# Token-major blocks computed in pairs of 512 columns, with the forward states scanned early, in an encoder layer of neighbourhood attention and gated linear attention

## The chip, the cores and the metric

The kernel runs on one core of a Trainium2 chip. The metric is the device time of one execution in microseconds. PE is TensorE, DVE is VectorE, ACT is ScalarE, POOL is GpSimd, SP is SyncE, whose queue issues nearly all DMAs.

## What is computed

One layer of a hybrid encoder for two sequences, a prompt P of 512 tokens and a sample S of 1024, in fp32, width 1024. The normalized input u is projected by one matrix w_in into eleven parts; the parts that matter here are

```
proj = u @ w_in + b_in
na_q, na_k, na_v (512 columns each)        # neighbourhood attention, 8 heads
gla_q, gla_k (256 each), gla_v, gla_g (512 each)   # gated linear attention, 4 heads
gate_na, gate_gla (1024 each)

# gated linear attention, forwards and (flipped) backwards, per head
state = chunk_decay * state + k_dec^T v          # one state per chunk of tokens
o     = (scores within the chunk) v + q_dec state
gla_o = rmsnorm(o) * silu(gla_g)
```

Neighbourhood attention, the two output projections, their gating, the output matrix and a squared-relu MLP follow.

## The kernel before

**Exactness.** Every matmul of a projection is done as three: each operand x is split into a rounded high part (ACT, `Ring.split` L51 or `split_act` L153) and a remainder (DVE, L52 or L154), and high x high, high x low and low x high are summed in psum.

**Two ways of projecting.** A channel-major unit (`dense_cm`, L225 to L227) holds 128 columns of weights as the stationary operand and streams 512 tokens: 24 matmuls of N = 512. A token-major unit (`dense_tm` with `tm_half`, L250 to L252) holds 128 tokens and streams a block of 256 weight columns: 24 matmuls of N = 256, for each of the 12 groups of 128 tokens (0 to 3 are P, 4 to 11 are S; 10 and 11 are done together). The token-major blocks in the stage are numbered: 4 and 5 are the two halves of gla_g, 1 the second half of gla_v, 2 and 3 the two halves of na_v.

**What follows a token-major unit**, `out_tm`: DVE adds the bias row out of psum into an sbuf tile `sv` (L316; the tag has two buffers). Block 1 is stored as it is. Blocks 2 and 3 are split into high and low (ACT L153, then DVE L154) into a tile `svr` or `svl`, one buffer each, chosen by the token group, and stored by two DMAs. Blocks 4 and 5 pass a silu on ACT (L332) and a multiplication on POOL (L334) and are stored to glag_d (L335). All of these DMAs are issued by SP.

**The weights** come through `Ring`: SP loads a [128x1024] raw tile (two buffers), ACT and DVE split it into a high and a low tile (three buffers each).

**The stage.** The list `mid` (L825 to L831) holds the units in their order: block 4, the channel-major weights k1 (the keys of the second pair of heads), blocks 1, 5, 2, 3, then the projections na (24 units) and the gates (24 units here). `run_dense` (L343 to L361) walks through it with a clock by hand: each group of three matmuls adds its cost (0.65 for N = 512, 0.325 for N = 256), and each time the clock passes 3.9 times the value that was last yielded, it lets the side generator `gla_all` issue its next piece. A finished unit's evacuation is issued a little later (`done`, `flush`).

**The side work**, `gla_all`, is the gated linear attention in two passes, one per pair of heads: segments of 512 tokens, 0P0, 0S0, 0S1, then 1P0, 1S0, 1S1. A visit to a segment (L771 to L803) is a loop over l = 0, 2, 4, 6, called a step here, each with four yields of 0.5: PE computes scores of two levels (L622; 16 matmuls a level), DVE merges them by a mask into `att` (`merge`, L660), and DVE prepares the operands Q and K of the next two levels (`ew`, L633 to L649). At the end of a segment the decayed keys are transposed (`kdt`, L694), multiplied with v into the states `st` (`upd`, L703). After the last segment of a sequence the states are chained by `scan` (L710 to L716, DVE, forward L715 and backward L716, in three thirds), and `out_mm` (L726, L727) multiplies scores and states. All of this goes into the same engines' queues in the order in which it is issued.

## Time and profile before

| | us |
|---|---|
| time, median of 3 runs (lowest to highest) | 2110.87 (2110.83 to 2110.98) |
| the profiled execution, its own time | 2112.74 |
| the profiled execution, its span | 2110.8 |
| PE busy (share of the span) | 2089.7 (99%) |
| DVE busy | 1318.2 (62%) |
| ACT busy | 974.9 (46%) |
| POOL busy | 64.5 (3%) |
| mean granted clock of PE | 0.998 |

The span is what lies between the first and the last instruction of the profile; the own time holds what lies around it too. Busy times overlap, since the engines work beside each other. The waits of an engine are told by what ended them; "L250 <- DVE sv L316" is a matmul of line 250 that waited for DVE's instruction of line 316.

### The profile page before, as it was taken

Reading aid. Unit: us, or ns where it says so; the run is one execution under the profiler, and the core shown is the slowest. Engines: PE = TensorE matmul, PEld = TensorE weight load, DVE = VectorE, ACT = ScalarE, POOL = GpSimd, SP = SyncE. Lnnn points to the kernel's source line nnn. Section 1 sums busy time; section 2 is a strip of 40 time slices with the busy share of each in tenths; the row PEclk is TensorE's granted clock in tenths of the full one; section 3 lists DMA queues with packets and bytes.
Section 4 is the critical chain, followed back from the end, with each engine's and each line's share of the span. In section 5 each row is a group of like instructions: output and inputs, shape, how many; then the busy total and the mean of one; then the engine's idle time right before and its main releaser. Section 6 shows DMA issues by size and latency. Waiting matters only on the chain.

```text
span 2110.8 us, 32043 instructions
## 1 busy us (share of the span) xinstructions
PE 2089.7 (99%) x11964; PEld 1890.3 (90%) x11964; DVE 1318.2 (62%) x2428; ACT 974.9 (46%) x1914; POOL 64.5 (3%) x92
## 2 busy tenths in 40 slices
PE   9999999999999999999999999999999999999998
PEld 8899998888888888898898999999999888888887
DVE  7465875767346666465576777997887444443544
ACT  6532232333345555452353666676666333333442
POOL 1020100000000000000000000000000000000000
PEclk9999999999999999999999999999999999999999
DMA  6342334564386776466666566766876755454643
GB/s 212 116 147 86 97 112 140 126 170 91 111 246 202 217 217 198 149 212 226 245 215 250 174 165 173 228 202 197 267 234 176 264 200 186 157 170 162 220 170 110
DMA packets 256426, 381.86 MB, mean 181 GB/s; under 512 B 35856, under 2 KB 163856, under 8 KB 256272
## 3 DMA queue, kind: packets, MB, share of 16 engines
q1 hardware_dynamic: 256128, 379.56, 57.5%
q8 instruction: 94, 1.54, 0.3%
q14 instruction: 60, 0.49, 0.1%
q10 hardware_dynamic: 144, 0.26, 0.0%
HBM read 256.02 MB, written 123.73 MB: 180 GB/s over the span
## 4 chain that ended last, share of the span: by engine, by line
PE 80%; DVE 2%; ACT 1%; DMA 1%; issue 1%; SPq 0%; POOLq 0%; DVEq 0%; ACTq 0%
PE psd L225 6%; PE psd L227 6%; PE psd L226 6%; PE psa L1426 4%; PE psa L1428 4%; PE psa L1427 4%; PE psa L1581 2%; PE psa L1580 2%; PE psa L1582 2%; PE psb L1580 2%; PE psb L1581 2%; PE psb L1582 2%; PE psc L1581 2%; PE psc L1580 2%; PE psc L1582 2%; PE psb L1428 2%
## 5 line engine op out<-in xcount | busy, mean ns | idle before, releaser
L154 DVE TENSOR_TENSOR al<-al,ah 128x1024 fp32r<-128x1024 f32 x82 | 100.2, 1223 | 145.7 <-ACT ah L153 135.2
L153 ACT ACTIVATE ah<-al 128x1024 fp32r<-128x1024 f32 x82 | 86.6, 1057 | 225.2 <-DMA al<-ads 134.3
L225 PE MATMUL psd<-uhiS,wh 128*128 128x512 f32 x448 | 179.6, 401 | 0.8 <-ACT st L287 0.8
L227 PE MATMUL psd<-uhiS,wl 128*128 128x512 f32 x448 | 175.3, 391 | 0.0
L226 PE MATMUL psd<-uloS,wh 128*128 128x512 f32 x448 | 174.8, 390 | 0.0
L1426 PE MATMUL psa<-c,uwh 128*128 128x384 f32 x512 | 171.7, 335 | 0.8 <-DVE xb L1366 0.7
L1428 PE MATMUL psa<-c,uwl 128*128 128x384 f32 x512 | 171.0, 334 | 0.0
L1427 PE MATMUL psa<-c,uwh 128*128 128x384 f32 x512 | 171.0, 334 | 0.0
L1331 DVE TENSOR_TENSOR uwl<-ux,uwh 128x512 fp32r<-128x512 f32 x192 | 131.0, 687 | 58.7 <-ACT uwh L1347 57.6
L1347 ACT ACTIVATE uwh<-ux 128x512 fp32r<-128x512 f32 x192 | 120.0, 626 | 79.6 <-DVE ux L1341 66.3
L52 DVE TENSOR_TENSOR wl<-wr,wh 128x1024 fp32r<-128x1024 f32 x70 | 85.5, 1223 | 105.2 <-ACT wh L51 94.1
L51 ACT ACTIVATE wh<-wr 128x1024 fp32r<-128x1024 f32 x70 | 73.8, 1056 | 143.9 <-PE psc L1231 66.0
L225 PEld LDWEIGHTS psd<-uhiS,wh 128*128 128x128 f32 x448 | 84.2, 188 | 18.3 <-ACT st L287 1.2
L227 PEld LDWEIGHTS psd<-uhiS,wl 128*128 128x128 f32 x448 | 84.1, 188 | 18.2
L226 PEld LDWEIGHTS psd<-uloS,wh 128*128 128x128 f32 x448 | 84.3, 188 | 16.1
L1426 PEld LDWEIGHTS psa<-c,uwh 128*128 128x128 f32 x512 | 96.1, 188 | 1.5 <-DVE xb L1366 1.0
L1427 PEld LDWEIGHTS psa<-c,uwh 128*128 128x128 f32 x512 | 96.1, 188 | 0.0
L1428 PEld LDWEIGHTS psa<-c,uwl 128*128 128x128 f32 x512 | 96.1, 188 | 0.0
L250 PE MATMUL psd<-wh,uhiS 128*128 128x256 f32 x320 | 92.7, 290 | 0.8 <-DVE sv L316 0.8
L251 PE MATMUL psd<-wl,uhiS 128*128 128x256 f32 x320 | 90.9, 284 | 0.0
L252 PE MATMUL psd<-wh,uloS 128*128 128x256 f32 x320 | 90.8, 284 | 0.0
L225 PE MATMUL psd<-uhiP,wh 128*128 128x512 f32 x224 | 90.3, 403 | 0.0
(557 smaller groups left out, 5889.4 us busy)
## 6 DMA issues: line engine op xcount, KB each, us to landing
ux<-in_wup_dram SPq DMA_DIRECT2D x64, 512.0 KB
al<-ads SPq DMA_DIRECT2D x48, 512.0 KB
al<-ad SPq DMA_DIRECT2D x34, 512.0 KB
bq<-t_d SPq DMA_DIRECT2D x64, 256.0 KB
wr<-in_wst_dram SPq DMA_DIRECT2D x28, 512.0 KB
gate_d<-st SPq DMA_DIRECT2D x48, 256.0 KB
sg<-gate_d SPq DMA_DIRECT2D x32, 384.0 KB
ad<-xa SPq DMA_DIRECT2D x64, 192.0 KB
```

What stands on the lines that cost most here:

```text
L154: V.tensor_tensor(lo, src, hi.bitcast(F32), op=ALU.subtract)
L225: T.matmul(p, wh, xh[:, k, sl], start=(k == 0), stop=False)
L226: T.matmul(p, wh, xl[:, k, sl], start=False, stop=False)
L227: T.matmul(p, wl, xh[:, k, sl], start=False, stop=(k == 7))
L1331: V.tensor_tensor(lo, usrc.pop(m - 1), hi.bitcast(F32), op=ALU.subtract)
L1347: A.activation(uhl[m][0], usrc[m], AF.Copy)
L1426: T.matmul(u[b], wh[:, es], c[:, 0, k], start=(new and k == 0), stop=False, skip_group_check=True)
L1427: T.matmul(u[b], wh[:, es], c[:, 1, k], start=False, stop=False, skip_group_check=True)
L1428: T.matmul(u[b], wl[:, es], c[:, 0, k], start=False, stop=(k == 3), skip_group_check=True)
L1580: T.matmul(p, ah[:, jj], bh[:, cs], start=((new or last) and jj == 0), stop=False, skip_group_check=True)
L1581: T.matmul(p, ah[:, jj], bl[:, cs], start=False, stop=False, skip_group_check=True)
L1582: T.matmul(p, al[:, jj], bh[:, cs], start=False, stop=(kh == 1 and jj == 7), skip_group_check=True)
```

## The change

The blocks (4, 5) and (2, 3) become two pairs (`dense_pair`): a unit holds 128 tokens and streams 512 weight columns, 24 matmuls of N = 512 (cost 0.68 per three), and when it ends, both blocks' evacuations are issued one after the other. Token groups 0 and 1 are done together, and 10 and 11. The order is k1 first, then pair (4, 5), pair (2, 3), then block 1, which stays as it was, and then the rest. The pairs' weights are loaded in sixteen pieces of [128x512] by ACT's queue, each split by `split_act` into one shared buffer: those of the first pair during k1 and in the first token groups, those of the second during the last two of the first pair (`next_pair`); in the last two of the second pair the ring is started again (`next_ring`). Ring is rebuilt on eight shared [128x1024] buffers, which the stages behind use too. The forward chain of states over the first four chunks (`scan_f`, three operations for each of two heads) is issued in the steps l = 4 and l = 6 of the second segment of S, and the scan leaves it out; its three yields go from 1.1, 0.9, 0.9 to 0.8, 0.8, 0.9. The four yields of a step go from 0.5 each to 0.46, 0.46, 0.46, 0.65. A few tiles find other places (the tile of zeros, the gate weights, the bias rows, now in three buffers).

```diff
-    def __init__(self, nc, raw, rawtag, nraw, pool, tag, nslots, items):
-        self.nc, self.raw, self.pool, self.items = nc, raw, pool, items
-        self.rawtag, self.tag, self.nraw, self.nslots = rawtag, tag, nraw, nslots
+    def __init__(self, nc, pool, nbuf, items):
+        self.nc, self.pool, self.items = nc, pool, items
+        self.free, self.limit, self.done = list(range(nbuf)), len(items), 0
         self.loaded, self.parts = [], []
+
+    def alloc(self, dt, name):
+        s = self.free.pop(0)
+        return s, self.pool.tile([128, 1024], dt, tag=f"w{s}", name=name)
 
     def load(self):
         i = len(self.loaded)
-        t = self.raw.tile([128, 1024], F32, tag=self.rawtag, bufs=self.nraw, name=f"{self.tag}r{i}")
-        self.nc.sync.dma_start(t, self.items[i])
-        self.loaded.append(t)
+        self.loaded.append(self.alloc(F32, f"wr{i}"))
+        self.nc.sync.dma_start(self.loaded[i][1], self.items[i])
 
     def split(self):
         i = len(self.parts)
-        t = self.loaded[i]
-        hi = self.pool.tile([128, 1024], F32R, tag=self.tag + "h", bufs=self.nslots, name=f"{self.tag}h{i}")
-        lo = self.pool.tile([128, 1024], F32R, tag=self.tag + "l", bufs=self.nslots, name=f"{self.tag}l{i}")
+        s, t = self.loaded[i]
+        (hs, hi), (ls, lo) = [self.alloc(F32R, f"w{c}{i}") for c in "hl"]
         self.nc.scalar.activation(hi, t, AF.Copy)
         self.nc.vector.tensor_tensor(lo, t, hi.bitcast(F32), op=ALU.subtract)
-        self.parts.append((hi, lo))
+        self.free.append(s)
+        self.parts.append((hs, ls, hi, lo))
+
+    def release(self, live):
+
+        while self.done < min(live, len(self.parts)):
+            self.free += self.parts[self.done][:2]
+            self.done += 1
 
     def fill(self, live):
 
-        n = len(self.items)
+        self.release(live)
         while True:
-            if len(self.loaded) < n and len(self.loaded) - len(self.parts) < self.nraw:
+            if len(self.loaded) < self.limit and len(self.loaded) - len(self.parts) < 2 and self.free:
                 self.load()
-            elif len(self.parts) < len(self.loaded) and len(self.parts) - live < self.nslots:
+            elif len(self.parts) < len(self.loaded) and len(self.parts) - self.done < 3 and len(self.free) > 1:
                 self.split()
             else:
                 return
 
-    def step(self, live):
-
-        if len(self.parts) < min(len(self.items), live + self.nslots):
-            if len(self.loaded) == len(self.parts):
-                self.load()
-            self.split()
-            if len(self.loaded) < len(self.items):
-                self.load()
-
     def get(self, i):
-        return self.parts[i]
+        return self.parts[i][2:]
...
-    def add_mv(b):
-        add(f"mv{b}", d["wmv"][2 * b], d["wmv"][2 * b + 1])
-
-    for n in ("q0", "k0", "q1"):
+    for n in ("q0", "k0", "q1", "k1"):
         add(n, d["wst"][ST[n]])
-    add_mv(4)
-    add("k1", d["wst"][3])
-    add_mv(1)
-    add_mv(5)
-    add_mv(2)
-    add_mv(3)
+    add("mv1", d["wmv"][0], d["wmv"][1])
     for i in range(8):
...
-    ring = Ring(nc, raw, "wraw", 2, rngp, "w", 3, items)
+    ring = Ring(nc, raw, 8, items)
+    ring.limit = where["mv1"]
...
-    zero = cst.tile([128, 128], F32, name="zero")
-    V.memset(zero, 0.0)
...
-        brow[b] = stg2.tile([128, 256], F32, tag="brow", name=f"brow{b}")
+        brow[b] = stg2.tile([128, 256], F32, tag="brow", bufs=3, name=f"brow{b}")
...
-            if i == 0:
+            if i == 4:
                 ring.fill(wi)
-            if b not in brow:
-                load_brow(b)
-            if i == 6 and TM.index(b) < 5:
...
+    PAIRS = ((4, 5), (2, 3))
+    pw = [dict(n=0, raw=[], parts={}) for _ in PAIRS]
+
+    def pw_load(q, n=1, s=None):
+
+        w = pw[q]
+        if s is not None:
+            b, x = ring.alloc(F32, f"pr{q}{w['n']}")
+        for e in range(n):
+            k = w["n"]
+            if s is None:
+                t = stg2.tile([128, 512], F32, tag=("svr", "svl")[k % 2], bufs=1, name=f"pr{q}{k}")
+                w["raw"].append((t, None))
+            else:
+                t = x[:, e * 512:e * 512 + 512]
+                w["raw"].append((t, b if e == n - 1 else None))
+            A.dma_start(t, d["wpr"][q, k])
+            w["n"] += 1
+
+    def pw_split(q):
+        w = pw[q]
+        k = len(w["parts"])
+        t, b = w["raw"].pop(0)
+        s, x = ring.alloc(F32R, f"pw{q}{k}")
+        split_act(x[:, :512], x[:, 512:], t)
+        w["parts"][k] = s, x
+        if b is not None:
+            ring.free.append(b)
+
+    def pw_ahead(mm, q):
+
+        def run():
+            for n, cost in enumerate(mm()):
+                yield cost
+                if n % 4 == 3:
+                    pw_split(q)
+                    pw_load(q)
+        return run
+
+    def dense_pair(q, i, evac, nxt=None):
+
+        def step(p, k, j):
+            x = pw[q]["parts"][k][1]
+            xh, xl = tok_ap(u_hi, k, j), tok_ap(u_lo, k, j)
+            T.matmul(p, xh, x[:, :512], start=(k == 0), stop=False)
+            T.matmul(p, xh, x[:, 512:], start=False, stop=False)
+            T.matmul(p, xl, x[:, :512], start=False, stop=(k == 7))
+
+        def end(p, j):
+            for e in range(2):
+                evac(p[:, e * 256:e * 256 + 256], PAIRS[q][e], j)
+
+        def mm():
+            if i == 0 and q == 0:
+                ring.release(where["k1"] + 1)
+            if i == 9 and nxt:
+                nxt(-1)
+            ii = (i, i + 1) if i in (0, 10) else (i,)
+            p = {}
+            for k in range(8):
+                for j in ii:
+                    if k == 0:
+                        if j == 1:
+                            flush()
+                        p[j] = ps("d")
+                    step(p[j], k, j)
+                    yield 0.68
+                    if k == 7:
+                        done.append(lambda j=j: end(p[j], j))
+                if i == 0:
+                    if k in (2, 4):
+                        pw_split(q)
+                    if k == 4:
+                        for b in PAIRS[q]:
+                            if b not in brow:
+                                load_brow(b)
+                if i == 6 and k == 0:
+                    load_brow(PAIRS[1][0] if q == 0 else 1)
+                if i == 10:
+                    ring.free.append(pw[q]["parts"][k][0])
+                    if nxt:
+                        nxt(k)
+        return mm
+
+    def next_pair(k):
+        if k == -1:
+            pw_load(1, 2)
+        elif k == 0:
+            pw_load(1, 2, 0)
+        elif k != 3:
+            pw_split(1)
+            if k in (1, 2, 6, 7):
+                pw_load(1)
+
+    def next_ring(k):
+        ring.limit = len(items)
+        if k in (0, 1):
+            ring.load()
+        elif k in (5, 7):
+            ring.split()
+            if k == 7:
+                ring.load()
 
...
-            r = stg2.tile([128, 4, 2, 64], F32R, tag=("svr", "svl")[i % 2], bufs=1, name=f"svr{uid[0]}")
+            r = stg2.tile([128, 4, 2, 64], F32R, tag=("svr", "svl")[(i + b) % 2], bufs=1, name=f"svr{uid[0]}")
...
+                gkw = p0.tile([128, 512], F32, tag="v0r", bufs=2, name="gkw")
...
+                load_brow(5)
...
+    zero = p0.tile([128, 4, 32], F32, tag="lrt", bufs=4, name="zero").rearrange("p a b -> p (a b)")
+    V.memset(zero, 0.0)
...
+        def scan_f(x, h):
+
+            st, cd = x["st"], x["cd"]
+            for c in range(1, 4):
+                V.scalar_tensor_tensor(out=st[0:64, h, c + 1], in0=st[0:64, h, c], scalar=cd[0:64, h, c:c + 1], in1=st[0:64, h, c + 1], op0=ALU.mult, op1=ALU.add)
...
-                    V.scalar_tensor_tensor(out=st[0:64, h, c + 1], in0=st[0:64, h, c], scalar=cd[0:64, h, c:c + 1], in1=st[0:64, h, c + 1], op0=ALU.mult, op1=ALU.add)
+                    if n == 4 or c > 3:
+                        V.scalar_tensor_tensor(out=st[0:64, h, c + 1], in0=st[0:64, h, c], scalar=cd[0:64, h, c:c + 1], in1=st[0:64, h, c + 1], op0=ALU.mult, op1=ALU.add)
...
-                yield 0.5
+                yield 0.46
                 if l == 0 and kd is not None:
                     kdt(kd, "ba")
+                if l == 4 and c0:
+                    scan_f(x, 0)
+                if l == 6 and c0:
+                    scan_f(x, 1)
...
-                yield 0.5
+                yield 0.46
...
-                yield 0.5
+                yield 0.46
...
-                yield 0.5
+                yield 0.65
...
-                    yield (1.1, 0.9, 0.9)[half] if x["n"] > 4 else 0.34
+                    yield (0.8, 0.8, 0.9)[half] if x["n"] > 4 else 0.34
...
-    mid += [dense_tm(4, i, out_tm) for i in range(12)]
-    for n_, dst, cb in (("k1", glak_d, 3),):
-        mid += [dense_cm(n_, seg, out_cm(dst, cb, 128, cb < 2)) for seg in range(3)]
-    for b in (1, 5, 2, 3):
-        mid += [dense_tm(b, i, out_tm) for i in range(12)]
+    pw_load(0, 2)
+    mid = [pw_ahead(dense_cm("k1", seg, out_cm(glak_d, 3, 128)), 0) for seg in range(3)]
+    for q, nxt in enumerate((next_pair, next_ring)):
+        mid += [dense_pair(q, i, out_tm, nxt) for i in (0, *range(2, 11))]
+    mid += [dense_tm(1, i, out_tm) for i in range(12)]
...
+                ring.release(wi + 1)
...
-                x = raw.tile([128, 1024], F32, tag="wraw", bufs=2, name=f"ux{p}{e}") if p % 2 == 0 else tmp(f"ux{p}{e}")
+                s, x = ring.alloc(F32, f"ux{p}{e}") if p % 2 == 0 else (None, tmp(f"ux{p}{e}"))
+                uslot.setdefault(p, []).append(s)
...
+                ring.free += [s for s in uslot.pop(p) if s is not None]
...
-                uhl["t"] = [rngp.tile([128, 1024], F32R, tag=f"w{c}", bufs=3, name=f"uw{c}{m}") for c in "hl"]
+                uslot["w", m + 1], uhl["t"] = zip(*[ring.alloc(F32R, f"uw{c}{m}") for c in "hl"])
...
+                    ring.free += uslot.pop(("w", n), ())
...
-    d["wmv"] = c(np.stack([stat(w[h * 512:(h + 1) * 512, m:m + 256]) for m in mv for h in range(2)]))
+    d["wmv"] = c(np.stack([stat(w[h * 512:(h + 1) * 512, gv + 256:gv + 512]) for h in range(2)]))
+    d["wpr"] = c(np.stack([w[:, m:m + 512].reshape(8, 128, 512) for m in (gg, nav)]))
```

## Rows read from the trace of the kernel before

**Rows 1.** The page, busy time of each engine, its share of the span and its instructions.

```profile
PE 2089.7 (99%) x11964; PEld 1890.3 (90%) x11964; DVE 1318.2 (62%) x2428; ACT 974.9 (46%) x1914; POOL 64.5 (3%) x92
```

**Rows 2.** The waits of PE from 108 to 560 us: what waited, for what, us in all, times, longest.

```profile
PE psa L727 <- DVE stt0S L716: 2.6, 1, 2.6
PE psa L622 <- DVE K0S L637: 1.8, 2, 1.1
PE psa L622 <- DVE K1S L637: 1.4, 1, 1.4
PE psd L250 <- DVE sv L316: 0.8, 1, 0.8
PE psa L622 <- DVE K1P L637: 0.5, 1, 0.5
PE psa L694 <- DVE att0S L657: 0.4, 1, 0.4
PE psb L703 <- ACT stt0S L708: 0.4, 1, 0.4
```

**Rows 3.** Windows: the stretch, its length, busy us (and instructions) of PE, PEld, DVE, ACT and POOL, the granted clock as a share, the DMA share, GB/s.

```profile
220.00:240.00 20.00, 20.00 (x197) 19.49 (x196) 18.80 (x36) 2.47 (x6) 4.22 (x5) 1.00 0.37 126
...
260.00:280.00 20.00, 19.56 (x181) 18.59 (x179) 18.25 (x32) 6.13 (x11) 2.05 (x2) 1.00 0.43 144
...
320.00:340.00 20.00, 16.64 (x124) 16.10 (x123) 10.78 (x30) 3.86 (x14) 0.81 (x1) 0.91 0.27 82
...
332.00:334.00 2.00, 2.00 (x11) 2.00 (x12) 0.69 (x2) 0.42 (x1) 0.00 (x0) 0.57 0.08 23
334.00:336.00 2.00, 2.00 (x12) 2.00 (x12) 0.00 (x0) 0.00 (x0) 0.00 (x0) 0.57 0.25 64
```

**Rows 4.** PE's groups by line and form from 108 to 560 us: the first of the three terms of each contraction block of the 256-column matmuls; busy us and mean ns, idle before.

```profile
L250 PE MATMUL psd<-wh,uhiS 128*128 128x256 f32 x320 | 92.7, 290 | 0.8 <-DVE sv L316 0.8
...
L250 PE MATMUL psd<-wh,uhiP 128*128 128x256 f32 x160 | 45.7, 286 | 0.0
```

**Rows 5.** PE's timeline, 256 columns, a stretch without a wait or an insertion: start, length, instruction. From the first row to the last there are 54 matmuls.

```profile
316.04 0.28 PE L250 MATMUL psd<-wh,uhiP 128*128 128x256 f32 x1
...
322.52 0.28 PE L250 MATMUL psd<-wh,uhiP 128*128 128x256 f32 x1
```

**Rows 6.** PE's timeline, 512 columns: the first matmul of a burst, two of it with 29 matmuls from the one to the other, and the score matmuls that end the burst.

```profile
387.60 0.50 PE L225 MATMUL psd<-uhiS,wh 128*128 128x512 f32 x1
...
389.10 0.39 PE L225 MATMUL psd<-uhiS,wh 128*128 128x512 f32 x1
...
395.67 0.39 PE L227 MATMUL psd<-uhiS,wl 128*128 128x512 f32 x1
395.99 2.06 PE L622 MATMUL psa<-Q1P,K1P 64*128 64x128 f32 x32
```

**Rows 7.** PE's timeline, visit 0S0: the 32 score matmuls that begin two steps in a row, and the first dense matmul of the first one's burst.

```profile
231.43 2.06 PE L622 MATMUL psa<-Q0S,K0S 64*128 64x128 f32 x32
...
233.41 0.39 PE L250 MATMUL psd<-wh,uhiS 128*128 128x256 f32 x1
...
242.24 2.06 PE L622 MATMUL psa<-Q0S,K0S 64*128 64x128 f32 x32
```

**Rows 8.** DVE's timeline in visit 0S1: start, length, instruction, in brackets idle before it and what ended it.

```profile
277.15 1.35 DVE L660 COPY_PREDICATED att0S<-msk,psa 128x512 f32<-128x512 uint8 x2
278.39 0.41 DVE L316 TENSOR_TENSOR sv<-psd,brow 128x256 f32<-128x256 f32 x1
279.34 0.43 DVE L154 TENSOR_TENSOR svr<-sv,svr 128x256 fp32r<-128x256 f32 x1 [0.53 <-ACT svr L153]
279.68 0.69 DVE L633 TENSOR_TENSOR Q0S<-q0S,Y0S 128x512 f32<-128x512 f32 x1
...
287.66 0.42 DVE L316 TENSOR_TENSOR sv<-psd,brow 128x256 f32<-128x256 f32 x1
288.95 1.35 DVE L660 COPY_PREDICATED att0S<-msk,psa 128x512 f32<-128x512 uint8 x2
```

**Rows 9.** PE's timeline in the same stretch: the scores of one step, 16 and 16.

```profile
278.83 1.16 PE L622 MATMUL psa<-Q0S,K0S 64*128 64x128 f32 x16
...
281.11 1.16 PE L622 MATMUL psa<-Q0S,K0S 64*128 64x128 f32 x16 [1.12 <-DVE K0S L637]
```

**Rows 10.** DVE's groups by line and form from 108 to 560 us: the sums that evacuate token-major blocks, and a chunk product.

```profile
L316 DVE TENSOR_TENSOR sv<-psd,brow 128x256 f32<-128x256 f32 x60 | 25.2, 420 | 43.6 <-PE psd L252 31.6 <-DMA glag_d<-sv 7.3 <-DMA glak_d<-st 3.7
...
L684 DVE TENSOR_TENSOR qd0S<-q0S,Y0S 64x512 f32<-64x512 f32 x4 | 3.7, 928 | 0.1
```

**Rows 11.** The scan: DVE's timeline (its first two operations and its last), and PE's two rows that waited.

```profile
318.33 0.34 DVE L715 SCALAR_TENSOR_TENSOR stt0S<-stt0S,cd0S 64x128 f32<-64x128 f32 x1
318.70 0.35 DVE L716 SCALAR_TENSOR_TENSOR stt0S<-stt0S,cd0S 64x128 f32<-64x128 f32 x1
...
331.45 0.35 DVE L716 SCALAR_TENSOR_TENSOR stt0S<-stt0S,cd0S 64x128 f32<-64x128 f32 x1
...
326.69 0.39 PE L250 MATMUL psd<-wh,uhiS 128*128 128x256 f32 x1 [0.78 <-DVE sv L316]
...
331.19 0.46 PE L727 MATMUL psa<-stt0S,qd0S 128*128 128x128 f32 x2 [2.58 <-DVE stt0S L716]
```

**Rows 12.** The only line of the kernel that issues a DMA from ACT: shortest, median and longest ns that the issue held the engine.

```profile
L1520 ACTq DMA_DIRECT2D out_dram<-xf x1: 395/395/395, 2107.3 to 2107.3; - x1
```

More of the change, by code (lines that the diff above doesn't have):

```diff
@@ L106, in tile_trunk @@
     raw = rnge.enter_context(tc.tile_pool(name="raw", bufs=1))
-    rngp = rnge.enter_context(tc.tile_pool(name="rng", bufs=1))
     banks = {}
@@ L237, in tile_trunk @@
     brow = {}
-    TM = (0, 4, 1, 5, 2, 3)
     def load_brow(b):
-        brow[b] = stg2.tile([128, 256], F32, tag="brow", name=f"brow{b}")
+        brow[b] = stg2.tile([128, 256], F32, tag="brow", bufs=3, name=f"brow{b}")
         SP.dma_start(brow[b], d["brow"][b])
@@ L260, in mm @@
         def mm():
-            if i == 0:
+            if i == 4:
                 ring.fill(wi)
-            if b not in brow:
-                load_brow(b)
-            if i == 6 and TM.index(b) < 5:
-                load_brow(TM[TM.index(b) + 1])
             if i == 11:
@@ L433, in norm_side @@
         SP.dma_start(gkb, d["gkb"])
-        gkw = p0.tile([128, 512], F32, name="gkw")
         xn = {}
@@ L823, in gla_all @@
                     yield 0.93
-    mid = []
-    mid += [dense_tm(4, i, out_tm) for i in range(12)]
-    for n_, dst, cb in (("k1", glak_d, 3),):
-        mid += [dense_cm(n_, seg, out_cm(dst, cb, 128, cb < 2)) for seg in range(3)]
-    for b in (1, 5, 2, 3):
-        mid += [dense_tm(b, i, out_tm) for i in range(12)]
+    pw_load(0, 2)
[3 more added lines that the diff above has]
+    mid += [dense_tm(1, i, out_tm) for i in range(12)]
     for i in range(8):
@@ L1300, in factors @@
         return out
-    uraw, uhl, useq = {}, {}, []
+    uraw, uhl, useq, uslot = {}, {}, [], {}
     for p in range(33):
```

## The prediction

> **What bounds the kernel now.** I read the page's busy times first, then TensorE's waits, then the windows of the stage that the change touches, then the timelines of PE and DVE inside it. The page gives PE 2089.7 of a span of 2110.8 us [rows 1]: the kernel is bound by TensorE, and only two things can move the time, the time that PE needs for its matmuls and the 21.1 us in which it doesn't work. In the stage from 108 to 560 us, where all changed work lies, PE waited 7.9 us [rows 2]; every one of these waits ends with VectorE (or with ScalarE behind it), none with a weight load or a store. The reader is to see in the windows [rows 3] that DVE is far from idle there: 18.80 of 20 us at 220 to 240, 18.25 at 260 to 280, against 62% over the whole span [rows 1]. And behind the longest wait, 2.6 us, the granted clock stands at 0.57 from 332 to 336 us [rows 2, 3], near the lower of the two levels, 1.2 of 2.4 GHz: 4 us at 0.57 do the work of 2.3, so that wait cost 1.7 us more, and the waits cost 9.6 in all.
>
> **Pairing, the gain.** Blocks 4, 5, 2 and 3 go from 256 to 512 columns a matmul. There are 480 first terms for five blocks [rows 4], so 96 for one and with three terms 288; four blocks are 1152 matmuls, which become 576. In an undisturbed stretch 54 matmuls of 256 columns lie between 316.04 and 322.52, 0.120 us each [rows 5]; 29 of 512 lie between 389.10 and 395.67, 0.2266 each [rows 6]. 1152 x 0.120 = 138.2, 576 x 0.2266 = 130.5: **-7.7 us**. A burst of matmuls restarts after each insertion of the visit's own: from 387.60 to 395.99 36 matmuls of 512 took 8.39, 0.23 over 36 x 0.2266 [rows 6]; from 233.41 to 242.24 72 of 256 took 8.83, 0.19 over 72 x 0.120 [rows 7]. Some 20 bursts at 0.04 more: **+0.8**.
>
> The rows give a gap beyond the columns of 0.120 - 256/2400 = 0.0133 at either width, and halving the number of matmuls saves one gap of two. The Trainium skill ("TensorE: Matmul & The Clock Gate", section "Back-to-back issue gap") states about 2.5 ns instead; by it 1152 would take 125.8 and 576 124.3, an estimate, so the pairing would gain only 1.5. The trace disagrees with its 13.3 ns, at both widths.
>
> **What the gain runs into.** A visit of the gated linear attention is four steps; in each PE does 32 score matmuls (2.06 us) and the dense matmuls that the clock of run_dense lets in. An unhindered step lasts 10.8 us now (231.43 to 242.24) [rows 7]. After the change a step is 0.46 x 3 + 0.65 = 2.03 of 3.9 units, 7.92; at 0.68 for three matmuls that is 34.9 matmuls, 7.92 us, plus 0.23 and the scores' 1.98 (start to start): 10.1. DVE's part of a step doesn't shrink with it. From 277.15 to 288.95, 11.8 us, DVE never rests but for ScalarE's answers [rows 8]: two merges of 1.24, two elementwise levels of 2.73, and three evacuations of a v block of 1.29 each (sum, 0.5 of idle until ScalarE's high part is there, remainder: the first from 278.39 to 279.68, the third from 287.66). That step was late on PE already: 1.12 us at 281.11 [rows 9]. The pair (2, 3) evacuates both blocks of a token in one go, so 7.92/5.44 = 1.46 tokens (24 matmuls x 0.2266 = 5.44) with two evacuations each: 3.75, and 7.95 + 3.75 = 11.7. So in every step beside the second pair **DVE needs 11.7 and PE 10.1**: PE will wait for elementwise results (L637) where it hardly waited before.
>
> Now by visits, PE's waits to come (low to high). A wait isn't paid twice: a lead that a visit starts with, or a psum buffer that decouples, lowers it, so I take values inside the bounds.
> - First visit (prompt, pair (4, 5)): its two evacuations a token are one sum each (0.42), the silu is ScalarE's; 0 to 1, taken 0.5.
> - Visit 0S0, three steps from first to fourth merge: DVE 7.5 (six merges) + 15.0 (five and a half levels) + 1.4 (sums of the first pair) + 5.2 (eight splits of the second pair's weights, 0.65 each, the spacing of [rows 8]) + 5.2 (four evacuations of tokens 0 and 1) = 34.3; PE 3 x 10.1 = 30.4. That is 3.9, and up to 3.8 more if a store holds a buffer (7.3 in two times of the sums' waits for glag_d before [rows 10]); taken 5.5.
> - From 0S0 to 0S1 DVE needs 11.3 for a step of PE of 9.75: 1.5 to 3.0, taken 2.
> - Visit 0S1: chunk work 4.6 (four products of queries of 0.7, one form up to 0.93 [rows 10], two of keys, and four small copies), merges 7.5, levels 15.0, the next segment's product 1.1, four tokens x 2 x 1.29 = 10.3: 38.5 against PE's 33.4; 4.4 to 5.5, taken 5.
> - The transposes and the update behind it: 0 to 1.1, taken 0.5.
> - The scan. 24 small DVE operations, spaced 0.37, stand between the update and the first output now, and the first output waited 2.58 for the last of them, with 0.78 just before [rows 11]: 3.4. The change does six of them early (beside the last steps of 0S1, where DVE is full, 2.2 us that I count in no gain) and gives the scan less cover: 2.5 units of clock for 2.9. DVE 18 x 0.37 + three tokens of two evacuations 7.7 = 14.4; PE 9.75 + 2.1 = 11.9; 2.6 to 5.6, taken 4.5. So moving a quarter of the scan gains nothing, as the pair's evacuations fill the place.
> - The visits of the second pair of heads lie beside channel-major work; only the last quarter of each step is 0.15 x 3.9 = 0.6 longer and the first three shorter: 0 to 2.3 for 1.9 before (1.4 + 0.5 [rows 2]), taken 1.0.
> - A wait of about 2.5 us was followed by a lower clock before and one of 1.1 wasn't [rows 3, 9]. Two such waits are likely (0S1 or 0S0, and the scan): 3.4, one to three: 1.7 to 5.1.
>
> Sum 0.5 + 5.5 + 2 + 5 + 0.5 + 4.5 + 1.0 + 3.4 = 22.4 (low 14.1 without all that is uncertain in it, high 31.3), for 9.6 now: **+12.8**.
>
> **Parts with little in them.** Sixteen weight loads go to ScalarE's queue. The only such issue in the trace held ScalarE 0.395 us [rows 12]: 16 x 0.395 = 6.3 us on an engine that is busy 2 to 6 of 20 us here [rows 3]. Behind a load in ScalarE's order stand the high parts of evacuations and weight splits; a load into a buffer still being read waits with all of them behind it (each reload follows its split's remainder on DVE). Below, 0; above, one such wait of a split's length at each of the ten splits that reload at once, 10 x 0.7 = 7; taken 0, since six of them lie beside channel-major work. The shared ring of eight buffers changes no PE wait that I find: none in this stage ends with a load [rows 2], so 0, with up to 1 either way. The order of k1 first, v block 1 last: no wait shows there. The new place of the tile of zeros, and the bias rows in three buffers: 0.
>
> **The sum.** -7.7 + 0.8 + 12.8 = +5.9. The profiled execution took 2112.74 about its span of 2110.8; the median of the three runs shown is 2110.87, 1.9 less. On the profiled one that is 2118.6, on the median 2116.8, **2117**. With the low waits it is -2.4 (2108.5), with the high ones +14.8 (2125.7).
>
> **Rivals.** A, *DVE keeps up and the pairing is left whole*. The sum of a token's second block can fill the 0.5 us in which DVE waits for ScalarE's high part of the first [rows 8], about 1.0 a token, and the ten tokens beside visits give 10 back; the waits then stay near 9.6 and the time is 2110.87 - 7.7 + 0.8 + 0 to 1 = 2104 to 2105. For it: ScalarE has room. Against: end() hands both blocks to out_tm one after the other, so in DVE's order the first's remainder stands ahead of the second's sum. It decides if a nav token takes DVE under 1.6. B, *a draw*: the waits come out at their low ends, spread over many short ones that don't lower the clock, 2108.5 to 2115, say 2111. For it: the short waits of 1.1 left the clock alone [rows 3, 9]. C, on the slow side beyond the forecast: *ScalarE's queue holds evacuations behind loads*, and the 7 above falls where DVE is late already: 2117 + 7 = 2124, say 2125. It decides if a reload is issued before its buffer's last reader has run. D, that the pairing doesn't do what it says: by the page's gap it gains 1.5 and not 7.7: 2117 + 6 = 2123; the spacing rows speak against it.
>
> **Chances.** Forecast (2113 to 2122) 0.42; A 0.25; B 0.25; C 0.06; D 0.02. Range: from A's 2104 to 2124, with the rest of C and the highest waits left out. A measurement of this kernel can tell about 0.2%, 4.2 us, from no change: under 2106.6 is faster (A, less a little: 0.23), over 2115.1 slower (most of the forecast, a third of it being near the bound, with C and D: 0.47), between them 0.30.
>
> **What the profile after would show.** Right: L622 <- DVE K0S among PE's waits at 8 us or more in all, spread over 0S0 and 0S1; DVE over 18 of 20 us there; L727 <- DVE stt0S still at 2 or more; a granted clock under 1 in more than one place; 0.227 a paired matmul. Rival A shows as a sum of the second block between the first block's sum and its remainder, and L622's waits under 3. C shows as ScalarE idle until a DMA of its own issue, with DVE waiting for it. Wrong I would be most of all about DVE's step of 11.7, if two evacuations in a row overlap; then the gain of 7 stays.

## The result

The changed kernel took 2124.51 us (2123.44 to 2126.4), the kernel before 2110.93 in the same comparison: a ratio of 1.0063 (95% interval 1.0051 to 1.0075), 13.6 us slower. Forecast were 2117 and a range of 2104 to 2124: the direction held, the size was more than double (13.6 for 5.9).

The page's busy times of the changed kernel, whose span is 2123.7 us, against [rows 1]:

```profile
PE 2090.7 (98%) x11388; PEld 1864.2 (88%) x11388; DVE 1315.5 (62%) x2436; ACT 975.9 (46%) x1922; POOL 63.0 (3%) x92
```

PE issues 576 matmuls fewer and yet is busy 1.0 us longer; the rest of the 12.9 that the span has grown is idle time, 33.0 for 21.1. PE's waits of the changed kernel from 108 to 560 us (what waited, for what, us in all, times, longest), against the 7.9 of [rows 2]:

```profile
PE psa L714 <- DVE K0S L729: 8.6, 3, 4.9
PE psd L239 <- ACT wh L53: 2.8, 1, 2.8
PE psa L703 <- issue: 2.1, 1, 2.1
PE psa L714 <- DVE Q0S L725: 2.1, 1, 2.1
PE psd L240 <- DVE wl L54: 1.4, 2, 0.7
PE psd L310 <- DVE sv L405: 1.1, 1, 1.1
PE psa L714 <- DVE K0P L729: 0.9, 1, 0.9
PE psd L311 <- DVE pw L146: 0.6, 1, 0.6
PE psa L795 <- ACT kd0S L788: 0.4, 1, 0.4
PE psa L714 <- DVE K1S L729: 0.4, 1, 0.4
PE psa L703 <- DVE qkl L146: 0.2, 1, 0.2
```

They sum to 20.6. The wait of 2.6 for the scan (L727 before) is gone. New are waits for weights: L239 and L240 are block 1's matmuls, waiting for the halves of its weights; L703 is the first product of the visits, whose "issue" hides a chain through ACT and DVE (below). The other surprise is the granted clock. Some of the windows of the changed kernel in which PE ran low, at least one of each stretch (stretch, length, busy us of PE, PEld, DVE, ACT, POOL, granted clock, DMA share, GB/s), against [rows 3]:

```profile
134.00:136.00 2.00, 1.89 (x18) 1.49 (x16) 1.87 (x6) 0.00 (x0) 0.00 (x0) 0.66 0.50 188
136.00:138.00 2.00, 2.00 (x7) 1.60 (x6) 2.00 (x5) 0.00 (x0) 0.00 (x0) 0.50 0.00 0
...
248.00:250.00 2.00, 1.11 (x10) 1.11 (x12) 1.93 (x5) 0.00 (x0) 0.00 (x0) 0.50 0.42 140
...
266.00:268.00 2.00, 2.00 (x7) 1.48 (x7) 2.00 (x4) 0.00 (x0) 0.00 (x0) 0.56 0.00 0
...
302.00:304.00 2.00, 2.00 (x13) 1.58 (x10) 0.69 (x1) 0.00 (x0) 0.00 (x0) 0.50 0.03 10
...
332.00:334.00 2.00, 2.00 (x11) 2.00 (x11) 0.00 (x0) 0.38 (x1) 0.00 (x0) 0.50 0.82 273
```

Five stretches at or near 0.5, the lower level (1.2 GHz), each behind a wait of 2 us or more, where the kernel before has one in this stage. This is the profiled execution, whose mean granted clock is 0.993; the other three runs of the changed kernel have 0.994 to 0.995, the kernel before 0.998. By these rounded means the clock held back 6 to 11 us more than before in each of the four runs, an estimate, where the forecast had 1.7 more (3.4 for 1.7).

Where the five waits come from is read from the timelines. ACT and DVE before the first product (start, length, instruction, in brackets idle before and what ended it), and PE's row:

```profile
127.95 0.63 ACT L145 ACTIVATE pw<-pr 128x512 fp32r<-128x512 f32 x1 [4.04 <-DMA pr<-in_wpr_dram]
129.34 0.33 ACTq L282 DMA_DIRECT2D pr<-in_wpr_dram  x1
129.73 0.69 ACT L376 ACTIVATE st<-psd,bcol 128x512 f32<-128x512 f32 x1 [1.14 <-DVE pw L146]
130.31 0.62 ACT L145 ACTIVATE pw<-pr 128x512 fp32r<-128x512 f32 x1
130.97 0.69 DVE L146 TENSOR_TENSOR pw<-pr,pw 128x512 fp32r<-128x512 f32 x1 [1.66 <-PE psd L217]
131.58 0.68 DVE L689 TENSOR_TENSOR qk<-q0P,k0P 128x512 f32<-128x512 f32 x1
...
133.02 0.50 PE L703 MATMUL psa<-qkh,two 64*128 64x512 f32 x2 [2.08 <-issue]
```

The product qk stands on DVE behind the remainder of a weight piece, that behind ACT's high part, that behind a k1 evacuation and a load's issue; and this issue waited for the remainder of the piece before, whose load ACT had waited 4.04 us for. The late operand at 249, DVE and ACT:

```profile
241.81 0.42 DVE L405 TENSOR_TENSOR sv<-psd,brow 128x256 f32<-128x256 f32 x1
244.31 0.42 ACT L145 ACTIVATE svr<-sv 128x256 fp32r<-128x256 f32 x1 [5.61 <-DMA nv_d<-svr]
244.76 0.43 DVE L146 TENSOR_TENSOR svr<-sv,svr 128x256 fp32r<-128x256 f32 x1 [2.54 <-ACT svr L145]
...
248.16 0.68 DVE L729 TENSOR_TENSOR K0S<-k0S,X0S 128x512 f32<-128x512 f32 x1
```

Token groups 0 and 1 end together, each fills both single buffers svr and svl, and the second's high part waits for the first's store to land. And block 1's weights, SP and ACT, and PE's longest wait for them:

```profile
305.94 12.46 SPq L419 DMA_DIRECT2D nv_d<-svr  x8
318.51 1.99 SPq L47 DMA_DIRECT2D wr<-in_wmv_dram  x2
323.11 1.06 ACT L53 ACTIVATE wh<-wr 128x1024 fp32r<-128x1024 f32 x1 [1.89 <-DMA wr<-in_wmv_dram]
...
328.40 0.42 ACT L145 ACTIVATE svr<-sv 128x256 fp32r<-128x256 f32 x1 [0.83 <-DVE sv L405]
328.73 1.04 ACT L53 ACTIVATE wh<-wr 128x1024 fp32r<-128x1024 f32 x1
...
329.82 0.58 PE L239 MATMUL psd<-wh,uhiP 128*128 128x256 f32 x1 [2.77 <-ACT wh L53]
```

SP issued the load only when the stores queued ahead of it had their data, and the first high part waited for it. The second high part, at 328.73, which PE's 2.77 waited for, did not wait for a load: it stands on ACT right behind the second high part of a token's evacuation, and that waited for DVE's sum. The other two waits end with DVE as well. Before the one of 3.06 at 301 DVE rests, from 266 on, only for ACT's answers. Before the one of 2.06 at 263 it had first waited for PE's matmul, and rested only for ACT's answers from there on:

```profile
257.51 0.42 DVE L405 TENSOR_TENSOR sv<-psd,brow 128x256 f32<-128x256 f32 x1 [1.58 <-PE psd L312]
```

### The profile page after: what moved, and what is told of

Read it like the earlier page. It is cut to its first block, busy times and chain, and to the rows that moved or that the text cites. A ratio compares the mean times of both kernels' runs of the same rounds, so it can differ in the third digit from the quotient of the medians.

```text
span 2123.7 us, 30929 instructions
## 1 busy us (share of the span) xinstructions
PE 2090.7 (98%) x11388; PEld 1864.2 (88%) x11388; DVE 1315.5 (62%) x2436; ACT 975.9 (46%) x1922; POOL 63.0 (3%) x92
## 4 chain that ended last, share of the span: by engine, by line
PE 89%; DVE 4%; DMA 3%; ACT 2%; issue 1%; SPq 0%; POOL 0%; POOLq 0%; ACTq 0%; DVEq 0%
PE psd L215 7%; PE psd L217 7%; PE psd L216 7%; PE psa L1531 4%; PE psa L1533 4%; PE psa L1532 4%; PE psa L1687 2%; PE psa L1688 2%; PE psa L1686 2%; PE psb L1686 2%; PE psb L1687 2%; PE psb L1688 2%; PE psc L1687 2%; PE psc L1686 2%; PE psc L1688 2%; PE psb L1533 2%
## 5 line engine op out<-in xcount | busy, mean ns | idle before, releaser
L54 DVE TENSOR_TENSOR wl<-wr,wh 128x1024 fp32r<-128x1024 f32 x62 | 75.8, 1223 | 123.9 <-ACT wh L53 111.4
L53 ACT ACTIVATE wh<-wr 128x1024 fp32r<-128x1024 f32 x62 | 65.3, 1055 | 134.1 <-PE psc L1333 64.3
L217 PE MATMUL psd<-uhiP,wl 128*128 128x512 f32 x224 | 87.7, 391 | 0.0
L216 PE MATMUL psd<-uloP,wh 128*128 128x512 f32 x224 | 87.4, 390 | 0.0
L1533 PE MATMUL psb<-c,uwl 128*128 128x384 f32 x256 | 85.5, 334 | 0.0
```

Of the source, the lines that this page charges most:

```text
L216: T.matmul(p, wh, xl[:, k, sl], start=False, stop=False)
L217: T.matmul(p, wl, xh[:, k, sl], start=False, stop=(k == 7))
L1533: T.matmul(u[b], wl[:, es], c[:, 0, k], start=False, stop=(k == 3), skip_group_check=True)
```

## The experiments

Theory T: the long waits come from places and orders (single buffers behind stores, weights behind a queue). Rival R: DVE is full beside the second pair, and the lack shows wherever it ends up. Two more questions: what the clock takes, and what the pairing gives in itself. Times are medians; the ratio is to the kernel before on the same chip (2111.2 to 2111.6 there). PE busy, span and waits are those of the one profiled execution, the waits PE's from 108 to 560 us; its own time lies below the median by 3.1 in e2, 3.9 in e5 and 1.9 in e7.

| run | us | ratio (95%) | PE busy, span | waits |
|---|---|---|---|---|
| changed kernel | 2124.51 | 1.0063 (1.0051 to 1.0075) | 2090.7, 2123.7 | 20.6 |
| e1 four buffers | 2122.38 | 1.0053 (1.0036 to 1.0070) | 2088.7, 2120.8 | 19.3 |
| e2 sums first | 2117.01 | 1.0025 (1.0015 to 1.0034) | 2085.1, 2112.2 | 14.6 |
| e3 ring on ACT | 2122.70 | 1.0051 (1.0036 to 1.0066) | 2087.0, 2121.4 | 21.0 |
| e4 first pieces early | 2119.55 | 1.0038 (1.0023 to 1.0053) | 2086.5, 2117.8 | 18.8 |
| e5 even quarters | 2131.12 | 1.0088 (1.0075 to 1.0102) | 2087.4, 2125.4 | 25.7 |
| e6 scan late | 2122.93 | 1.0053 (1.0039 to 1.0066) | 2087.0, 2121.4 | 21.2 |
| e7 all four of e1 to e4 | 2103.58 | 0.9959 (0.9947 to 0.9972) | 2078.8, 2099.9 | 8.4 |
| e8 changed, unpaired | 2126.50 | 1.0067 (1.0052 to 1.0083) | 2095.9, 2124.8 | 16.0 |
| e9 e7 without sums first | 2115.30 | 1.0023 (1.0014 to 1.0032) | 2085.6, 2114.5 | 15.8 |
| e10 e7, unpaired | 2106.52 | 0.9979 (0.9970 to 0.9989) | 2087.2, 2104.8 | 4.9 |
| e11 e7, scan late | 2105.68 | 0.9975 (0.9965 to 0.9984) | 2081.6, 2104.4 | 9.7 |
| e12 e7, even quarters | 2106.56 | 0.9978 (0.9969 to 0.9988) | 2082.2, 2105.1 | 10.2 |

**e1, four buffers.** In out_tm, for blocks 2 and 3 (shortened):

```diff
-        r = stg2.tile([128, 4, 2, 64], F32R, tag=("svr", "svl")[(i + b) % 2], bufs=1)
+        r = (stg.tile([128, 512], F32R, tag="st") if b == 2 else stg2.tile([128, 512], F32R, tag=("svr", "svl")[i % 2], bufs=1))
+        # the sum is written into r[:, :, 1], where the remainder stands later
```

> The changed kernel with the tile that na_v's high and low parts are stored from in four places instead of two: the sum is written where the remainder later stands, block 2 in the tag st and block 3 in svr or svl. Nothing of the arithmetic is left out. In the changed kernel DVE stood 2.54 us at 244.76 for a high part that ACT could not write, since the store of the token before had not landed, and PE then waited 4.86 at 248.89 with the clock at half for some 6 us behind it. Theory T (buffers and late weights make the long waits): that DVE stall is gone, the wait at 248.89 falls to about 2.3 and the drop behind it shrinks or goes: 2124.5 - 2.5 - 1.5 to 3.5, that is 2118 to 2121. Rival R (DVE is full, the stall only shows where the lack ends up): the wait moves to the next scores, under 1 us is won, 2123 to 2125.

PE's wait at 249 fell from 4.9 to 2.8, as T said for its half; the waits at 133 (2.9), 263 and 301 stayed. By the medians it gives 2.1 us, between the two theories; by the intervals there is no clear difference from the changed kernel.

**e2, sums first.** `end()` of the second pair issues both sums, both high parts, both remainders, then the stores (shortened):

```diff
-            for e in range(2):
-                evac(p[:, e * 256:e * 256 + 256], PAIRS[q][e], j)
+            ts = [tm_sum(p[:, e * 256:e * 256 + 256], b) for e, b in enumerate(bs)]
+            for t, r in zip(ts, rs): A.activation(high(r), t, AF.Copy)
+            for t, r in zip(ts, rs): V.tensor_tensor(low(r), t, high(r), op=ALU.subtract)
```

> The changed kernel with a token's two na_v evacuations interleaved: both sums, both high parts, both remainders, then the stores; the same work in another order, the two st and the svr and svl buffers as before. It takes away the idle 0.5 us before each remainder (10 to 12 tokens x 2 x 0.5 = 10 to 12 us of DVE's order in the stretch of the second pair). Rival R (DVE full in 0S0 and 0S1 is the cause): DVE's step falls from 11.7 to about 10.3 against PE's 10.1, the L714 <- DVE K0S waits fall from 8.6 to 3 to 5 and with them a clock drop: 2116 to 2119. Theory T: the waits at 248.9 (store) and at 325 to 331 (weights) stay; only that at 301 falls, 3 us and a drop of 1.5: 2119 to 2121.

7.5 us, R's size. The wait at 301 is gone and the one at 263 is 1.2. The one behind the store stays, 3.9 long. So each theory has its own places. (The first product's wait is 0.7 in this profile, without a drop, though the edit does not touch it.) DVE and ACT of e2 in the same visit; "x2" is both blocks in one row, the remainders start 0.95 after the sums, and the store still holds the second token group:

```profile
233.96 0.74 DVE L408 TENSOR_TENSOR sv<-psd,brow 128x256 f32<-128x256 f32 x2
234.91 0.76 DVE L420 TENSOR_TENSOR svr<-sv,svr 128x256 fp32r<-128x256 f32 x2 [0.21 <-ACT svr L417]
...
238.32 0.75 DVE L408 TENSOR_TENSOR sv<-psd,brow 128x256 f32<-128x256 f32 x2
241.74 0.72 ACT L417 ACTIVATE svr<-sv 128x256 fp32r<-128x256 f32 x2 [6.53 <-DMA nv_d<-svr]
242.19 0.76 DVE L420 TENSOR_TENSOR svr<-sv,svr 128x256 fp32r<-128x256 f32 x2 [3.12 <-ACT svr L417]
```

**e3, block 1's weights on ACT's queue**, in `next_ring`:

```diff
-            ring.load()
+            ring.load(A)      # A.dma_start in place of SP's
```

> The changed kernel with the two loads of block 1's weights in next_ring (k = 0 and 1) issued by ACT's queue instead of SP's, where they stood behind the stores of the token groups before (the first load issued at 318.5). Theory T: block 1's high and low parts come earlier, the waits of 0.68 at 325, 2.77 at 329.8 and 0.68 at 331 shrink by 3 to 4 us and the drop at 330 to 336 (about 3 us) goes: 2118 to 2121. Rival R: the splits stand behind DVE's evacuations anyway, the waits stay or turn into one of out_mm for the scan (L727 of the kernel before, 2.6 us): 2123 to 2125.

ACT's first split came at 321.6 instead of 323.1, the waits for block 1 fell from 4.2 to 2.7 and the stretch at half clock behind them is gone, but a wait of 1.0 for the scan appeared: between the two. So SP's queue accounts for 1.5 of the 4.2 us; the 2.7 that are left stand behind a token's evacuation on ACT and DVE. Alone the edit is not clearly distinct from the changed kernel.

**e4, the first pair's pieces early:**

```diff
     pw_load(0, 2)
+    pw_load(0, 2, 0)
...
                     pw_split(q)
-                    pw_load(q)
+                    if len(pw[q]["parts"]) in (1, 2, 5, 6):
+                        pw_load(q)
```

> The changed kernel with four instead of two of the first pair's weight pieces loaded ahead of k1 (two into a free ring buffer), the reloads after the first, second, fifth and sixth split. In the changed kernel the first product of the visits (DVE, 131.58) stood behind the seventh and eighth split's wait for its load, PE waited 2.08 and 0.18 for it at 133 and ran at half clock from 134 to 138. Theory T: those 2.3 us and the 1.7 to 2 of clock come back: 2120 to 2121. Rival R: DVE's late start here is taken up by slack in the first visit; the wait stays at 2 because the product waits for glaq's and the gates' loads from SP: 2124 to 2125.

The wait at 133 and its half clock are gone, 5.0 us by the medians: T, and a little more than it said; the two intervals just touch. The waits behind stayed as they were, so the first visit had no slack to lend.

**e5, even quarters** (0.5 four times) in the changed kernel:

> The changed kernel with the four quarters of a step at 0.5 each again (2.00 in all for 2.03). Theory T/R alike (the buffers, the weights and DVE's load make the waits, not the yields): a step of PE is 0.1 us shorter and the last quarter's cover 0.6 less, so the waits on L714's operands grow by 0.3 to 0.6 a step that is late, 2124 to 2127. Rival: the short first three quarters bring the scores too early, and with even quarters the waits at 249 and 301 shrink by some 1 us each: 2121 to 2123.

6.6 us slower by the medians, more than either said: the three K0S waits grew from 8.6 to 13.5. **e6, the early scan taken out** (the two calls of `scan_f`):

> The changed kernel with the six forward state updates back in the scan (24 operations there), with the new shorter yields kept. They are 2.2 us of DVE, three at 292.44 just before the late scores at 301.34 and three at 307. By my prediction's step that moving them gains nothing: the wait at 301 falls by 1.1 and a wait of 1 to 2 for the last state update appears at the first output, 2123.5 to 2125.5. Rival (the early scan is what removed the wait of 2.6 that the kernel before had there): a wait of 2.5 or more comes back at the first output with a clock drop, 2127 to 2129.

No slower: the K0S waits fell from 8.6 to 6.4, the longest for block 1's weights grew from 2.8 to 4.5, since their splits now stand behind six more scan operations on DVE. No wait for the scan came back, as block 1's weights hide it.

**e7, all four.**

> The changed kernel with all four edits of the first runs: four tiles for na_v's parts, both sums first, block 1's weights on ACT's queue, four pieces of the first pair ahead. Alone they gave 2.1, 7.5, 1.8 and 5.0 us. If each takes away waits of its own (theory T), the sum is 16.4 and the time 2108; if DVE is full and some of the lack only moves (rival R), the waits in 0S0 and at the first output keep 6 to 8 us and the time is 2111 to 2114. Granted clock: one or two drops left by R, at most one by T.

2103.58, T's side and beyond: the four gave 20.9 where they gave 16.4 one by one. One by one each left waits of 2 us or more and drops behind them; that this is all of the 4.5 was not shown. It beats the kernel before by 0.41%. Its page and some of its waits; no window of 2 us from 100 to 560 is under a clock of 0.99:

```profile
PE 2078.8 (99%) x11388; PEld 1855.2 (88%) x11388; DVE 1314.8 (63%) x2436; ACT 974.4 (46%) x1922; POOL 63.1 (3%) x92
```

```profile
PE psa L749 <- DVE K0S L764: 2.1, 3, 1.0
...
PE psa L749 <- DVE Q0S L760: 1.5, 1, 1.5
...
PE psd L239 <- ACT wh L53: 0.9, 1, 0.9
```

As e7 issues the same 11388 matmuls as the changed kernel, the difference of their PE busy times, 2090.7 - 2078.8 = 11.9, is what the clock took in the whole execution. But 1.7 of it, by the windows from 10 to 18 us, lies at the start of the execution. There the profiles of the changed kernel, of the kernel before and of e10 have a stretch at half clock, 1.7 each, and e7's has none, though e7 and e10 are one program up to the pairs. One window each of the changed kernel, of e7 and of e10:

```profile
12.00:14.00 2.00, 2.00 (x10) 2.00 (x10) 1.55 (x2) 1.79 (x6) 0.87 (x2) 0.50 0.43 166
```

```profile
12.00:14.00 2.00, 1.55 (x10) 1.08 (x8) 1.55 (x2) 1.56 (x4) 1.13 (x2) 1.00 0.44 174
```

```profile
14.00:16.00 2.00, 1.83 (x9) 1.49 (x9) 1.56 (x2) 0.34 (x2) 1.16 (x1) 0.50 0.00 0
```

So in the stage the clock took 10.2 us of PE's time. The stage's windows of 2 us under full clock, (1 - clock) x 2 us each, sum to 12.0, of it 3.4 for the stretches at 249 and at 330 and 1.7 for each of the others; the part above 10.2 fell into time in which PE was waiting anyway.

**e8 and e10, unpaired** in the changed kernel and in e7 (shortened):

```diff
-            T.matmul(p, xh, x[:, :512], ...)   # and the other two terms
+            for e in range(2):
+                T.matmul(p[:, e*256:e*256+256], xh, x[:, e*256:e*256+256], ...)   # and the other two
```

> The changed kernel with the pairs' matmuls in two halves of 256 columns (1152 matmuls for 576), same weights, order, yields and evacuations. By the spacing rows this gives PE 7.7 us more work. If PE sets the time in all of these stretches, 2124.5 + 7 = 2131 to 2132. If DVE sets it in 0S0 and 0S1 (the forecast's reason), PE's slower pace there fills its own waits: of the 7.7 some 3 to 5 are hidden, and with a step of 10.8 for DVE's 11.7 the waits get shorter and a drop or two goes: 2121 to 2127.

(In e8 both halves' first matmuls carry `start`, in e10 only the first half's. By my reading the second `start` begins the first half's sum anew, so that e8 leaves out its first contraction block; number and order of the instructions are as said.) e8 is 2.0 slower by the medians, within the intervals, with waits of 16.0 for 20.6: most of the pairing's gain had been spent on waiting.

> The version with four edits, its pairs' matmuls in two halves of 256 columns (1152 for 576), all else the same. With PE nearly without waits (8.4 us, no drop) the spacing rows' 7.7 less 0.8 of restarts should show almost whole: 2103.6 + 5 to 7, 2108.5 to 2110.5; in the changed kernel as it stands the same edit cost 2.0. If the pairing is worth only 1.5 (a gap of 2.5 ns), 2105.

By its time, 2.9 slower than e7 by the medians (4.2 by the ratios, whose intervals overlap a little), e10 lies between the two expectations. PE's busy time decides: 2087.2 is 8.4 more than e7's 2078.8, 1.7 of it is the clock at the start, and 6.7 is left for the matmuls. In the stage e10 waits 3.5 less: even with the four edits DVE takes back about half of what the pairing gives.

**e9, e7 without sums first:**

> The version with four edits (2103.6) without the second: four tiles, block 1's weights on ACT's queue and four early pieces, but each na_v evacuation ends before the next begins, 0.5 us of idle DVE before each remainder. Rival R (DVE full in 0S0 and 0S1 is a cause of its own): the waits of L714's operands come back to 5 to 8 us with one to three drops, 2112 to 2118. Theory T (places and weights were the cause): 2104 to 2107.

11.7 slower than e7: R. The waits of L722's operands come back with stretches at half clock:

```profile
PE psa L722 <- DVE K0S L737: 6.7, 3, 3.2
PE psa L722 <- DVE Q0S L733: 2.1, 1, 2.1
```

**e11 and e12**, the early scan and the uneven quarters undone in e7:

> The version with four edits with the six forward state updates back in the scan. In the changed kernel that edit gave 1.6, as three of them stand before a late operand. Here 0S1 has no long wait: if the early scan is needed for the outputs, a wait on stt0S of 1 to 2.5 us appears, 2105 to 2108; if not, 2102.5 to 2104.

> The version with four edits with quarters of 0.5. In the changed kernel even quarters cost 6.6 us, of them 4.9 in longer waits for K0S. If that was because DVE was late already, they cost less here, 1 to 3 (2104.5 to 2106.5); if the last quarter's cover is needed in itself, 5 to 7 again (2108.5 to 2110.5).

e11 is 2.1 slower, but not by a wait on the state: L239's wait grows from 0.9 to 2.6, block 1's splits being behind more scan operations, and a stretch at half clock follows it (0.50 from 312 to 316). e12 is 3.0 slower, with a wait of 2.2 for K0S and a drop behind it; if that is right, half of what even quarters cost in the changed kernel was that DVE was late already. The intervals of both overlap e7's a little.

## Why the prediction was wrong

Term by term, from the waits above:

| term | taken (bounds) | measured |
|---|---|---|
| PE's matmuls, pairing with restarts | -6.9 | -6.7 (e10 to e7), -7.5 (before to e7), each without what the clock took |
| first visit | 0.5 (0 to 1) | 3.2 (2.1 + 0.2 + 0.9) |
| 0S0 | 5.5 (3.9 to 7.7) | 7.3 (1.1 + 0.6 + 0.7 + 4.9) |
| 0S0 to 0S1 | 2 (1.5 to 3.0) | 2.1 |
| 0S1 | 5 (4.4 to 5.5) | 3.1 |
| transposes, update | 0.5 (0 to 1.1) | 0.4 |
| scan and outputs | 4.5 (2.6 to 5.6) | 0 for the scan, 4.2 for block 1's weights |
| second pair of heads | 1.0 (0 to 2.3) | 0.4 |
| all waits | 19.0 | 20.7 |
| half clock | 3.4 (1.7 to 5.1) | 12.0 by windows, 10.2 of PE's time |

**The main reason held.** DVE needs more than PE in the steps beside the second pair. From 278.24 to 291.20 the changed kernel's DVE has two merges, two levels and two tokens, 12.96 us without a rest but for ACT's answers (the merges' rows that begin and end it):

```profile
278.24 1.35 DVE L752 COPY_PREDICATED att0S<-msk,psa 128x512 f32<-128x512 uint8 x2
...
291.20 1.34 DVE L752 COPY_PREDICATED att0S<-msk,psa 128x512 f32<-128x512 uint8 x2
```

The working gives the same: 7.95 and two tokens of 2.58 are 13.1. The stop of a store that the 0S0 term held open (3.8 more at most) came as 2.5. The pairing's gain came as taken, within 0.6, and its spacing of 0.2266 came out to the digit (6.57 over 29 matmuls, the rows below). The sum of the waits was right within 2 us, but partly by luck: the first visit and block 1 brought 2.7 and 4.2 that the terms did not hold, the scan and 0S1 6.4 less than they held.

```profile
138.44 0.39 PE L310 MATMUL psd<-pw,uhiP 128*128 128x512 f32 x1
...
145.01 0.39 PE L312 MATMUL psd<-pw,uloP 128*128 128x512 f32 x1
```

**The step that failed** is the term of the clock: "Two such waits are likely (0S1 or 0S0, and the scan): 3.4, one to three: 1.7 to 5.1." There were five, two of which cost 3.4 each, not 1.7: 12.0 by the forecast's own count of windows, 6.9 above the upper bound, and 10.2 of PE's time. That is most of the 7.0 by which the profiled span grew more than forecast (12.9 for 5.9). The three waits on DVE's results that the terms from 0S0 to 0S1 did expect (249, 263, 301) alone brought 6.8 by that count. The other two drops stand behind waits at two of my zeros. The loads on ScalarE's queue, "taken 0, since six of them lie beside channel-major work": they do, but the first product of the visits stands behind their remainders on DVE; 2.3 of waiting and 1.7 of clock (e4 gives 5.0 back). And the ring, "0, with up to 1 either way": the old ring's loads were never late, but I had not followed SP's queue, where the new first load stands behind eight stores that wait for DVE, nor the place of the splits behind a token's evacuation on ACT and DVE; 4.2 of waiting and 3.4 of clock, of which e3, by the queue alone, takes away 1.5 and the 3.4. Rival C had the right mechanism for the first and priced it at 7 without its place; that its 2124 to 2125 is the measured time is chance.

**Rival A named the right place but not enough of it**: "if a nav token takes DVE under 1.6", 2104 to 2105. In the changed kernel a token takes 2.5; in e7 1.63, from the sum to the next merge, and the time is 2103.6. In e2 it takes 1.63 too, with a time of 2117, and without it the other three edits give 2115.3 (e9): the condition was needed and did not do it alone. The rival that the pairing gains 1.5, an estimate by the gap of the Trainium skill ("TensorE: Matmul & The Clock Gate", section "Back-to-back issue gap"), falls: e10 shows 6.7 of PE time for it. That section gives the gap for an isolated matmul, and says that in a stream of weight loads and matmuls both set the spacing; here every matmul has its weight load (PEld x11388 beside PE x11388).

"Moving a quarter of the scan gains nothing" held in the changed kernel (e6); in e7 it gains 2.1 by the medians (e11), by way of block 1's splits. The uneven quarters, which I gave a word, are worth 6.6 here (e5) and 3.0 in e7. A reason could be that the shorter quarters bring merges earlier and that the longest cover stands before the next scores; no run separates the two.

## What to carry to other kernels

When one engine is at 99%, work taken from it shows up as time only if the second engine's order has room in that very stretch; count both per step, and count the idle time between dependent instructions as the second engine's work, since interleaving two chains gave the most room of the four edits here (7.5 us, e2). Follow each moved load through the queue that issues it, past every store that waits for data there. And where a wait lowers the clock, price waits by what lies behind them too: here some 13 us of new waiting (20.7 for 7.9) took 8.5 us more of clock (10.2 for 1.7).

## What the runs showed of the hardware

That a wait lowers the clock, and by how much, is not fixed by its length. In the changed kernel PE waited 2.08 and 0.18 at 133 and ran at 0.50 from 136 to 138. In e3 it waited as long at the same place, in e6 longer, and the clock stayed up (PE's rows of e3 and its window, then those of e6):

```profile
134.02 0.49 PE L703 MATMUL psa<-qkh,two 64*128 64x512 f32 x2 [2.20 <-issue]
134.70 0.50 PE L703 MATMUL psa<-qkl,two 64*128 64x512 f32 x2 [0.18 <-DVE qkl L146]
```

```profile
136.00:138.00 2.00, 2.00 (x17) 1.63 (x14) 1.97 (x5) 0.00 (x0) 0.00 (x0) 1.00 0.01 3
```

```profile
134.19 0.50 PE L703 MATMUL psa<-qkh,two 64*128 64x512 f32 x2 [2.50 <-issue]
```

```profile
136.00:138.00 2.00, 2.00 (x18) 1.66 (x15) 1.97 (x5) 0.00 (x0) 0.00 (x0) 1.00 0.00 0
```

And behind the wait of 4.9 at 249 the changed kernel's windows lose 3.4, behind one of 5.1 at the same place e3's lose 1.7. So what the clock takes at one place differs from run to run, and the costs by place above are those of single profiled executions. What decides it was not shown.
